# Block products from the third pair of column tiles on, with the products of the weights' own blocks first in a stage

## The chip, the core and the metric

The kernel runs on one core of a Trainium2 chip. The metric is the device time of one execution in microseconds (us). Four compute engines appear below: TensorE (PE, matrix products into the PSUM banks), VectorE (DVE), ScalarE (ACT) and GpSimd (POOL); SyncE (SP) issues most transfers. Each engine works through its own list of instructions in order and waits on semaphores for the others.

## What is computed

A trunk of two layers on 512 tokens of 1024 features, all in float32. Each layer is a half-step feed-forward block, a mixer (dilated attention and a convolution module, gated and merged) and a second half-step feed-forward block, each with an RMS norm ahead of it, and a final norm. The change is in the feed-forward blocks, of which there are four:

```python
def swiglu_ffn(h, w_up, w_down):
    a, b = jnp.split(h @ w_up, 2, axis=-1)
    return (jax.nn.silu(a) * b) @ w_down
...
    for l in range(DEPTH):
        x = x + 0.5 * swiglu_ffn(rmsnorm(x, ffn1_norm[l]), ffn1_w_up[l], ffn1_w_down[l])
        x = x + mixer(rmsnorm(x, mix_norm[l]), w_in[l], b_in[l], q_norm[l], k_norm[l],
                      w_attn_proj[l], conv_w[l], conv_b[l], conv_ln_g[l], conv_ln_b[l],
                      w_conv_proj[l], b_conv_proj[l], w_out[l], cos, sin)
        x = x + 0.5 * swiglu_ffn(rmsnorm(x, ffn2_norm[l]), ffn2_w_up[l], ffn2_w_down[l])
        x = rmsnorm(x, final_norm[l])
```

w_up is 1024 x 5632 (2816 columns for a, 2816 for b), w_down 2816 x 1024.

## The kernel before

**Number format.** PE multiplies in fp32r. To keep float32 accuracy each float32 matrix is split into a rounded part (hi, made by ACT) and the rest (lo, made by DVE as source less hi: L153 for a normal stage of weights, L167 elsewhere), and each product is three: hi x hi, hi x lo and lo x hi (`mm3`, L157 to L159). The activations are split once for a block, into xgh and xgl of eight k-tiles each.

**A feed-forward block** (`ffn`, L313) goes through the 22 column tiles of a and of b (128 columns each) in pairs m = 0, 2, 4, ..., in three parts of 8, 8 and 6 tiles; after each part come the products with w_down (ps_d). For each pair it needs the a half (two PSUM tiles ps_a) and the b half (two tiles ps_b, or the output o of a block product), then multiplies ps_a by R (the norm's factor, L338), applies Silu, multiplies by the b half (L341, L343) and splits the result into h.

**A normal pair** (`proj_cols`): two stages of weights of 512 KB, 48 products of 512 columns.

**A block product** (`proj7`, L282): the two column tiles and each pair of k-tiles form a 2 x 2 block matrix; the token halves (256 columns) and the k-tiles form the other one. Seven products of sums of blocks take the place of eight, so 84 products of 256 columns do the work of those 48. It too comes in two stages of 512 KB (`stage7`), each with two pairs q of k-tiles: DVE forms four sums of weight blocks (sm, L251 to L253), ACT rounds the raw block and the sums (hi, L166), DVE forms both rests (lo, L167). Of the seven products, numbers 0, 1 and 3 use the weights' own blocks, 2, 4, 5 and 6 their sums. They accumulate in four PSUM banks, given in `home`; at the end ACT and DVE combine the banks (L301 to L305). Before the change the b half of every pair but m = 0 is such a block product, and there it comes ahead of the a half: 10 in a feed-forward block, 40 in all.

**The sums of the activations** that the block products need are prepared once at the start of each `ffn`: DVE adds xgh and xgl again (L322, tile g), forms sums (`sums7`, L269 to L271, tile ts), ACT rounds them (Th) and DVE forms the rest (Tl). 

**The join of two stages.** At the end of a block the sums of squares of its output are added up over the partitions on PE (ps_ss, L198), made into a factor on DVE and ACT, spread by DVE onto a diagonal matrix dg (L212) and broadcast by PE (ps_bc, L214), from which ACT makes R (L220). ps_ss and ps_bc share one PSUM bank. Between the layers there are two ps_bc: the second one holds the final norm's factor, by which DVE rescales the eight x tiles within the next `ffn` (`deferred`, L778, called after pair m = 0). The pool of an `ffn` takes the memory that the pool before it gives back, dg's included.

**Buffers.** PSUM: three banks for ps_a (ps_mm), four for ps_b and the block products (ps_at), one for ps_ss and ps_bc (ps_st). Raw weights have two buffers, hi and lo four each, sm two.

**Order.** A tile scheduler that simulates a timeline fixes each engine's list when the program is built; stages of weights have a raised priority. What the list says is kept on the chip: an engine does not pass an instruction that waits.

In the code after the change, lines from L311 on have moved by one or two: L322 is L324, L338 is L340, L343 is L345, L778 is L780; of the block product's output, L301 to L305 are L302 to L306.

Of the kernel before, what the change touches and what calls it, by code (L numbers as in the profile page):

```python
# [44 lines left out]
def trunk(ctx: ExitStack, tc: tile.TileContext, A: dict, out: bass.AP):  # L45
# [8 lines left out]
    def ps_mm(name):  # L54
        return psp.tile([P, S], F32, tag="mm", name=name, bufs=3)

    def ps_st(name):
        return psp.tile([P, S], F32, tag="st", name=name, bufs=1)

    def ps_at(name):  # L60
        return psp.tile([P, S], F32, tag="at", name=name, bufs=4)
# [74 lines left out]
    def uniq(s):  # L136
        cnt[0] += 1
        return f"{s}_{cnt[0]}"
# [17 lines left out]
    def mm3(ps, ah, al, bh, bl, first, last):  # L156
        nc.tensor.matmul(ps, ah, bh, start=first, stop=False)  # L157
        nc.tensor.matmul(ps, ah, bl, start=False, stop=False)  # L158
        nc.tensor.matmul(ps, al, bh, start=False, stop=last)  # L159
# [80 lines left out]
    def stage7(pool, src):  # L240

        nk = src.shape[1]
        q = nk // 2
        m = nk * 256
        raw = wp.tile([P, 1024], F32, tag="raw", name=uniq("raw"), bufs=2)
        sm = pool.tile([P, 1024], F32, tag="sm", name=uniq("sm"), bufs=2)
        with tc.high_priority(offset=150):
            nc.sync.dma_start(raw[:, :m].rearrange("p (a n) -> p a n", a=nk), src)
            rv = raw[:, :m].rearrange("p (q e n) -> p e q n", q=q, e=4)
            sv = sm[:, :m].rearrange("p (e q n) -> p e q n", q=q, e=4)  # L250
            nc.vector.tensor_add(sv[:, 0:2], rv[:, 0::3], rv[:, 1][:, None].to_broadcast([P, 2, q, P]))  # L251
            nc.vector.tensor_add(sv[:, 2], sv[:, 1], rv[:, 0])
            nc.vector.tensor_add(sv[:, 3], sv[:, 2], rv[:, 2])  # L253
            f = []
            for t in (raw, sm):
                hi = wp.tile([P, 1024], F32R, tag="hi", name=uniq("hi"))
                lo = wp.tile([P, 1024], F32R, tag="lo", name=uniq("lo"))
                split_to(hi[:, :m], lo[:, :m], t[:, :m])
                p = "p (q e n) -> p e q n" if t is raw else "p (e q n) -> p e q n"
                f.append([x[:, :m].rearrange(p, q=q, e=4) for x in (hi, lo)])  # L260
        (rh, rl), (sh, sl) = f
        return [(rh[:, 0], rl[:, 0]), (rh[:, 2], rl[:, 2]), (sh[:, 3], sl[:, 3]), (rh[:, 3], rl[:, 3]),
                (sh[:, 1], sl[:, 1]), (sh[:, 2], sl[:, 2]), (sh[:, 0], sl[:, 0])]

    def sums7(pool, t2, h2, tag, bufs):

        tv = t2.rearrange("p k (h n) -> p (k h) n", h=2)
        w = pool.tile([P, 4, HT], F32, tag="w4", name=uniq("ts"), bufs=3)
        nc.vector.tensor_sub(w[:, 0:2], tv[:, 0::3], tv[:, 1:2].to_broadcast([P, 2, HT]))  # L269
        nc.vector.scalar_tensor_tensor(w[:, 2], w[:, 0], -1.0, tv[:, 3], op0=ALU.mult, op1=ALU.subtract)  # L270
        nc.vector.scalar_tensor_tensor(w[:, 3], w[:, 2], -1.0, tv[:, 2], op0=ALU.mult, op1=ALU.subtract)  # L271
        th = pool.tile([P, 4, HT], F32R, tag=tag, name=uniq("Th"), bufs=bufs)
        tl = pool.tile([P, 4, HT], F32R, tag=tag, name=uniq("Tl"), bufs=bufs)
        split_to(th, tl, w)

        def part(k, h):
            return tuple(x[:, h * HT:(h + 1) * HT] for x in h2[k])

        return [part(0, 0), part(1, 0), part(1, 1), (th[:, 3], tl[:, 3]),
                (th[:, 0], tl[:, 0]), (th[:, 2], tl[:, 2]), (th[:, 1], tl[:, 1])]  # L280

    def proj7(pool, src, c0, rhs, odd):  # L282

        if odd:
            bk = [ps_mm(uniq("ps_7")) for _ in range(3)] + [ps_st(uniq("ps_7"))]
        else:
            bk = [ps_at(uniq("ps_7")) for _ in range(4)]
        bv = [x.rearrange("p (h n) -> p h n", h=2) for x in bk]

        home = [(0, 0), (1, 0), (3, 0), (3, 1), (2, 0), (1, 1), (2, 1)]  # L290
        nq = len(rhs)
        for q0 in range(0, nq, 2):
            n_ = min(2, nq - q0)
            w = stage7(pool, src[:, 2 * q0:2 * (q0 + n_), c0:c0 + 256])
            for q in range(n_):
                for i in (0, 1, 5, 4, 6, 2, 3):
                    b, h = home[i]
                    mm3(bv[b][:, h], w[i][0][:, q], w[i][1][:, q], *rhs[q0 + q][i], q0 + q == 0 and h == 0, q0 + q == nq - 1 and (h == 1 or b == 0))
        o = pool.tile([P, 4, HT], F32, tag="w4", name=uniq("o7"), bufs=3)
        s1 = pool.tile([P, HT], F32, tag="s1", name=uniq("s1"), bufs=2)  # L300
        nc.scalar.activation(s1, bv[0][:, 0], AF.Copy)  # L301
        nc.vector.tensor_add(o[:, 0::3], bv[1], s1[:, None].to_broadcast([P, 2, HT]))  # L302
        nc.vector.tensor_add(o[:, 1:3], bv[2], o[:, 3:4].to_broadcast([P, 2, HT]))
        nc.vector.tensor_add(o[:, 3], bv[2][:, 0], o[:, 2])
        nc.vector.tensor_add(o[:, 1:3], bv[3], o[:, 1:3])  # L305
        return o.rearrange("p (k h) n -> p k (h n)", k=2)  # L306

    PARTS = ((0, 8), (8, 16), (16, 22))  # L311

    def ffn(l, w_up, w_down, xg, R, after, deferred=None):  # L313
        wu = w_up[l].rearrange("(k p) n -> p k n", p=P)
        wd = w_down[l].rearrange("(k p) n -> p k n", p=P)
        with tc.tile_pool(name=uniq("ffn"), bufs=4) as fp:
            few.add(id(fp))
            x7 = []
            for q in range(0, KD, 2):
                t2 = fp.tile([P, 2, S], F32, tag="t2", name=uniq("g2"), bufs=2)  # L320
                for j in range(2):
                    nc.vector.tensor_add(t2[:, j], xg[q + j][0].bitcast(F32), xg[q + j][1].bitcast(F32))  # L322
                x7.append(sums7(fp, t2, xg[q:q + 2], "T", 8))
            for m0, m1 in PARTS:  # L324
                h = []
                for m in range(m0, m1, 2):
                    pss = {}
                    for ab in ((0, 1) if m == 0 else (1, 0)):
                        if ab == 1 and m > 0:
                            o = proj7(fp, wu, FF + m * P, x7, False)  # L330
                            pss[1] = [o[:, 0], o[:, 1]]
                            continue
                        pss[ab] = [ps_mm(uniq("ps_a")) if ab == 0 else ps_at(uniq("ps_b")) for _ in range(2)]
                        proj_cols(wu, ab * FF + m * P, xg, KD, pss[ab])
                    t2 = fp.tile([P, 2, S], F32, tag="t2", name=uniq("t2"), bufs=2)
                    for j in range(2):
                        t = t2[:, j]
                        nc.vector.tensor_mul(t, pss[0][j], R)  # L338
                        nc.scalar.activation(t, t, AF.Silu)
                        if m > 0 and j == 1:  # L340
                            nc.vector.scalar_tensor_tensor(t, pss[1][j], -1.0, t, op0=ALU.mult, op1=ALU.mult)  # L341
                        else:
                            nc.vector.tensor_mul(t, pss[1][j], t)  # L343
                    h2 = split_to(*(fp.tile([P, 2, S], F32R, tag="h", name=uniq("h" + x), bufs=8) for x in "hl"), t2)
                    for j in range(2):  # L345
                        h.append(tuple(x[:, j] for x in h2))
                    if m == 0 and deferred is not None:
                        deferred()
                last = m1 == NF

                def take(k, src, f):
                    t = fp.tile([P, S], F32, tag="tmp", name=uniq("t"), bufs=5)
                    nc.vector.scalar_tensor_tensor(t, src, f, R, op0=ALU.mult, op1=ALU.mult)
                    nc.vector.tensor_add(xs[k], xs[k], t)
                    if last:
                        after(k, fp)

                wm = wd[:, m0:m1]
                for ts in ((0, 1), (2, 3), (4, 5), (6,), (7,)) if last else ((0, 1), (2, 3), (4, 5), (6, 7)):
                    pss = [(ps_at if ts[0] in (0, 4, 7) else ps_mm)(uniq("ps_d")) for _ in ts]  # L360
                    proj_cols(wm, ts[0] * P, h, m1 - m0, pss)
                    for k, ps in zip(ts, pss):
                        take(k, ps, 0.5)
# [492 lines left out]
```

## Time and profile before

| | us |
|---|---|
| median of 3 runs | 2684.32 (2680.71 to 2684.96) |
| the profiled execution | 2684.63 |
| its span | 2682.6 |
| PE busy in it | 2603.5 (97%) |
| DVE busy | 2018.0 (75%) |
| ACT busy | 1110.8 (41%) |
| mean granted clock of PE | 0.984 |

The busy time of an engine is the time in which it executes an instruction; PE's matmuls are pipelined, so the distance from one start to the next says more than the duration of one. The granted clock is the share of full speed that PE was given: 1.00 is 2.4 GHz, 0.50 is 1.2 GHz. In rows of the timeline, a bracket at the end tells how long the engine idled before the instruction and which instruction ended the idling. In rows, `ps` is a bank of a block product.

### The profile page before, as it was taken

What the parts mean: (1) busy time and instruction counts of PE and PEld (TensorE: products, weight loads), DVE (VectorE), ACT (ScalarE), POOL (GpSimd) and SP (SyncE); (2) the same over time, 40 slices, a digit from 0 to 9 for tenths busy, and PEclk for the clock granted to TensorE, in tenths of its full rate; (3) what the DMA queues carried; (4) which work ended last, traced back from release to release, by engine and by line L of the source; (5) the groups of instructions that cost most, each with busy time, mean ns of one, the idle gap of its engine ahead of it and who ended that gap; (6) DMA issues with size and microseconds to landing.
All of it is one profiled execution on the core that took longest, in us unless ns stands there. A gap on an engine that the chain in (4) does not pass through costs nothing.

```text
span 2682.6 us, 34833 instructions
## 1 busy us (share of the span) xinstructions
PE 2603.5 (97%) x13565; PEld 2180.7 (81%) x13565; DVE 2018.0 (75%) x3266; ACT 1110.8 (41%) x1664; POOL 110.7 (4%) x208
## 2 busy tenths in 40 slices
PE   7999999998999999999979999999989999999999
PEld 6888988776777778888858889887767778788887
DVE  6666669999986667666776666699999866676665
ACT  5333342243587234242433333422445873342334
POOL 1000000011011000000000000000010110000000
PEclk9999999999999999999989999999989999999999
DMA  3323233242333323232313232333323333232332
GB/s 126 114 91 108 85 114 106 80 121 88 107 108 113 114 79 103 87 112 92 104 47 110 87 111 90 111 103 91 110 86 119 111 124 106 63 118 87 110 94 79
DMA packets 245604, 268.89 MB, mean 100 GB/s; under 512 B 11624, under 2 KB 230128, under 8 KB 245440
## 3 DMA queue, kind: packets, MB, share of 16 engines
q1 hardware_dynamic: 233920, 234.91, 28.4%
q0 software_dynamic: 11504, 31.76, 4.0%
q8 instruction: 106, 1.74, 0.3%
q14 instruction: 58, 0.48, 0.1%
q10 hardware_dynamic: 16, 0.00, 0.0%
HBM read 251.75 MB, written 14.88 MB: 99 GB/s over the span
## 4 chain that ended last, share of the span: by engine, by line
PE 88%; DVE 10%; ACT 1%; issue 1%; DMA 0%; SPq 0%; DVEq 0%; ACTq 0%
PE ps_a L159 6%; PE ps_d L157 6%; PE ps_d L159 6%; PE ps_d L158 6%; PE ps_a L158 6%; PE ps_a L157 6%; PE ps L158 5%; PE ps L159 5%; PE ps L157 5%; PE ps_n L158 4%; PE ps_n L157 3%; PE ps_n L159 3%; DVE cv L618 2%; PE ps_S L526 1%; PE ps_pv L556 1%; PE ps_cp L158 1%
## 5 line engine op out<-in xcount | busy, mean ns | idle before, releaser
L152 ACT ACTIVATE hi<-raw 128x1024 fp32r<-128x1024 f32 (+1 forms) x368 | 378.5, 1039 | 611.5 <-PE ps_d L158 148.5
L153 DVE TENSOR_TENSOR lo<-raw,hi 128x1024 fp32r<-128x1024 f32 (+1 forms) x368 | 438.9, 1202 | 232.6 <-ACT hi L152 231.4
L618 DVE SCALAR_TENSOR_TENSOR cv<-u,cwc,cv 128x497 f32<-128x497 f32 (+14 forms) x480 | 339.0, 747 | 0.0
L157 PE MATMUL ps_a<-xgh,hi 128*128 128x512 f32 x704 | 275.1, 392 | 2.1 <-ACT xgh L174 2.1
L159 PE MATMUL ps_a<-xgh,lo 128*128 128x512 f32 x704 | 275.0, 392 | 1.8 <-DVE lo L153 1.8
L158 PE MATMUL ps_a<-xgl,hi 128*128 128x512 f32 x704 | 276.2, 392 | 0.1
L158 PE MATMUL ps_d<-hl,hi 128*128 128x512 f32 x704 | 272.6, 389 | 0.0
L159 PE MATMUL ps_d<-hh,lo 128*128 128x512 f32 x704 | 272.6, 389 | 0.0
L157 PE MATMUL ps_d<-hh,hi 128*128 128x512 f32 x704 | 270.6, 389 | 0.0
L158 PE MATMUL ps_n<-lo,xgh 128*128 128x512 f32 x576 | 229.0, 398 | 4.8 <-DVE lo L153 4.8
L159 PE MATMUL ps_n<-hi,xgl 128*128 128x512 f32 x576 | 226.0, 393 | 0.0
L157 PE MATMUL ps_n<-hi,xgh 128*128 128x512 f32 x576 | 215.0, 395 | 3.8 <-DVE tmp L481 3.8
L157 PE MATMUL ps<-Th,hi 128*128 128x256 f32 x640 | 182.3, 288 | 6.4 <-ACT Th L166 5.9
L158 PE MATMUL ps<-Tl,hi 128*128 128x256 f32 x640 | 183.9, 288 | 4.3 <-DVE Tl L167 4.3
L159 PE MATMUL ps<-Th,lo 128*128 128x256 f32 x640 | 182.0, 286 | 0.0
L166 ACT ACTIVATE hi<-sm 128x1024 fp32r<-128x1024 f32 x80 | 84.8, 1060 | 213.5 <-DVE sm L253 95.8
L159 PEld LDWEIGHTS ps_a<-xgh,lo 128*128 128x128 f32 x704 | 132.7, 189 | 31.1 <-DVE lo L153 3.1
L157 PEld LDWEIGHTS ps_a<-xgh,hi 128*128 128x128 f32 x704 | 133.0, 189 | 28.9 <-ACT xgh L174 2.5
L158 PEld LDWEIGHTS ps_a<-xgl,hi 128*128 128x128 f32 x704 | 132.8, 189 | 27.2 <-DVE xgl L175 0.8
L159 PEld LDWEIGHTS ps_d<-hh,lo 128*128 128x128 f32 x704 | 132.1, 188 | 27.5
L157 PEld LDWEIGHTS ps_d<-hh,hi 128*128 128x128 f32 x704 | 132.1, 188 | 27.4
L158 PEld LDWEIGHTS ps_d<-hl,hi 128*128 128x128 f32 x704 | 132.1, 188 | 27.4
(266 smaller groups left out, 5578.7 us busy)
## 6 DMA issues: line engine op xcount, KB each, us to landing
raw<-in_ffn_w_up_dram SPq DMA_DIRECT2D x176, 512.0 KB, 3.5
raw<-in_w_in_dram SPq DMA_DIRECT2D x88, 512.0 KB, 3.7
raw<-in_ffn_w_down_dram SPq DMA_DIRECT2D x76, 512.0 KB, 3.4
raw<-in_w_in_dram SPq DMA_DIRECT2D x96, 256.0 KB, 3.1
raw<-in_w_conv_proj_dram SPq DMA_DIRECT2D x16, 512.0 KB, 3.5
raw<-in_w_out_dram SPq DMA_DIRECT2D x16, 512.0 KB, 3.5
vd<-tmp POOLq DMA_DIRECT2D x24, 256.0 KB, 2.7
od<-ot POOLq DMA_DIRECT2D x24, 256.0 KB, 3.0
```

Source lines behind the costliest of these rows:

```text
L152: nc.scalar.activation(hi[:, :m], raw[:, :m], AF.Copy)
L153: nc.vector.tensor_sub(lo[:, :m], raw[:, :m], hi[:, :m].bitcast(F32))
L157: nc.tensor.matmul(ps, ah, bh, start=first, stop=False)
L158: nc.tensor.matmul(ps, ah, bl, start=False, stop=False)
L159: nc.tensor.matmul(ps, al, bh, start=False, stop=last)
L166: nc.scalar.activation(hi, src, AF.Copy)
L526: nc.tensor.matmul(pS[e][:, w * n + lo:w * n + hi], qkT[hp, i, b * P:(b + 1) * P], qkT[hp, 2 + i, k0 + lo:k0 + hi], start=True, stop=True)
L556: nc.tensor.matmul(pv[e * 64:(e + 1) * 64, i, b - b2, :], V[b + j][:, (hh * UH + h) * HD:(hh * UH + h + 1) * HD], PT[e][:, (nj * w + j) * ...
L618: nc.vector.scalar_tensor_tensor(a[:, t0:t1], u[k][:, t0 + d:t1 + d], cw(l, j, k), a[:, t0:t1], op0=ALU.mult, op1=ALU.add)
```

## The change

A constant M7 = 4 is added. In `ffn` the pairs m < 4 now are normal (the a half first, then the b half into ps_b), and block products begin at m = 4: 9 in a feed-forward block, 36 in all. The sign that goes with a block product's second tile (L341) follows. In `proj7` the loops within a stage are exchanged: the block products' number i runs outside, in the order 0, 1, 3, 5, 4, 6, 2, and the two pairs q of k-tiles run inside; which product opens and which closes a bank's accumulation follows. The transfers of weights on SP stay the same in number and order.

```diff
@@ -292,10 +292,11 @@
         for q0 in range(0, nq, 2):
             n_ = min(2, nq - q0)
             w = stage7(pool, src[:, 2 * q0:2 * (q0 + n_), c0:c0 + 256])
-            for q in range(n_):
-                for i in (0, 1, 5, 4, 6, 2, 3):
-                    b, h = home[i]
-                    mm3(bv[b][:, h], w[i][0][:, q], w[i][1][:, q], *rhs[q0 + q][i], q0 + q == 0 and h == 0, q0 + q == nq - 1 and (h == 1 or b == 0))
+
+            for i in (0, 1, 3, 5, 4, 6, 2):
+                b, h = home[i]
+                for q in range(n_):
+                    mm3(bv[b][:, h], w[i][0][:, q], w[i][1][:, q], *rhs[q0 + q][i], q0 + q == 0 and i in (0, 1, 3, 4), q0 + q == nq - 1 and i in (0, 5, 6, 2))
         o = pool.tile([P, 4, HT], F32, tag="w4", name=uniq("o7"), bufs=3)
         s1 = pool.tile([P, HT], F32, tag="s1", name=uniq("s1"), bufs=2)
         nc.scalar.activation(s1, bv[0][:, 0], AF.Copy)
@@ -308,6 +309,7 @@
 
 
 
+    M7 = 4
     PARTS = ((0, 8), (8, 16), (16, 22))
 
     def ffn(l, w_up, w_down, xg, R, after, deferred=None):
@@ -325,8 +327,8 @@
                 h = []
                 for m in range(m0, m1, 2):
                     pss = {}
-                    for ab in ((0, 1) if m == 0 else (1, 0)):
-                        if ab == 1 and m > 0:
+                    for ab in ((0, 1) if m < M7 else (1, 0)):
+                        if ab == 1 and m >= M7:
                             o = proj7(fp, wu, FF + m * P, x7, False)
                             pss[1] = [o[:, 0], o[:, 1]]
                             continue
@@ -337,7 +339,7 @@
                         t = t2[:, j]
                         nc.vector.tensor_mul(t, pss[0][j], R)
                         nc.scalar.activation(t, t, AF.Silu)
-                        if m > 0 and j == 1:
+                        if m >= M7 and j == 1:
                             nc.vector.scalar_tensor_tensor(t, pss[1][j], -1.0, t, op0=ALU.mult, op1=ALU.mult)
                         else:
                             nc.vector.tensor_mul(t, pss[1][j], t)
```

Three places in the engines' lists follow. The number behind a tile's name only tells instances apart.

PE at the feed-forward block 1 of layer 1, first block product (banks ps_1876, ps_1877) and the two ps_bc, before:

```order
L157 MATMUL ps_1876_11335<-xgh_10930,hi_11345 128x256
L158 MATMUL ps_1876_11335<-xgl_10931,hi_11345 128x256
L159 MATMUL ps_1876_11335<-xgh_10930,lo_11346 128x256
L214 MATMUL ps_bc_11133<-dg_11128,ones 128x512
L214 MATMUL ps_bc_11142<-dg_11137,ones 128x512
L157 MATMUL ps_1876_11335<-xgh_11006,hi_11401 128x256
L158 MATMUL ps_1876_11335<-xgl_11007,hi_11401 128x256
L157 MATMUL ps_1877_11336<-Th_11155,hi_11349 128x256
L159 MATMUL ps_1876_11335<-xgh_11006,lo_11402 128x256
```

There the two stand next to each other, 9 products into the block product. After, at the second normal pair (ps_b_11276 its fourth tile, ps_a_11214 its second):

```order
L157 MATMUL ps_b_11276<-xgh_10745,hi_11278 128x512
L158 MATMUL ps_b_11276<-xgl_10746,hi_11278 128x512
L159 MATMUL ps_b_11276<-xgh_10745,lo_11279 128x512
L214 MATMUL ps_bc_11020<-dg_11015,ones 128x512
L157 MATMUL ps_b_11276<-xgh_10808,hi_11278 128x512
L158 MATMUL ps_b_11276<-xgl_10809,hi_11278 128x512
...
L158 MATMUL ps_b_11276<-xgl_10974,hi_11308 128x512
L159 MATMUL ps_b_11276<-xgh_10973,lo_11309 128x512
L157 MATMUL ps_a_11214<-xgh_10734,hi_11216 128x512
L158 MATMUL ps_a_11214<-xgl_10735,hi_11216 128x512
L159 MATMUL ps_a_11214<-xgh_10734,lo_11217 128x512
```

The second ps_bc stood behind 9 products of the block product and now stands among the products of the second normal pair's b half; ps_a_11214 comes behind both ps_b tiles.

DVE at the same place, before (dg of the second ps_bc, the weights' sums, the activations' g, the rescales of x):

```order
L212 TENSOR_SCALAR dg_11137<-ident,rsr_11112 128x128 x4
L251 TENSOR_TENSOR sm_11340<-raw_11339 128x512
L322 TENSOR_TENSOR g_1841_11148<-xgh_10856,xgl_10857 128x512
L322 TENSOR_TENSOR g_1841_11148<-xgh_10867,xgl_10868 128x512
L322 TENSOR_TENSOR g_1845_11159<-xgh_10930,xgl_10931 128x512
L322 TENSOR_TENSOR g_1845_11159<-xgh_10943,xgl_10944 128x512
L251 TENSOR_TENSOR sm_11396<-raw_11395 128x512
L778 SCALAR_TENSOR_TENSOR x_81<-x_81,pcol,ps_bc_11142 128x512
L778 SCALAR_TENSOR_TENSOR x_82<-x_82,pcol,ps_bc_11142 128x512
```

The first operation of the new pool is there the weights' sum sm_11340. After:

```order
L212 TENSOR_SCALAR dg_11015<-ident,rsr_10990 128x128 x4
L153 TENSOR_TENSOR lo_11309<-raw_11307,hi_11308 128x1024
L324 TENSOR_TENSOR g_1821_11026<-xgh_10734,xgl_10735 128x512
L324 TENSOR_TENSOR g_1821_11026<-xgh_10745,xgl_10746 128x512
L324 TENSOR_TENSOR g_1825_11037<-xgh_10808,xgl_10809 128x512
L324 TENSOR_TENSOR g_1825_11037<-xgh_10821,xgl_10822 128x512
L251 TENSOR_TENSOR sm_11353<-raw_11352 128x512
L780 SCALAR_TENSOR_TENSOR x_81<-x_81,pcol,ps_bc_11020 128x512
L780 SCALAR_TENSOR_TENSOR x_82<-x_82,pcol,ps_bc_11020 128x512
```

One sum of weights (sm) ahead of the activations' g has gone behind them, and a rest (lo) of a normal stage stands there.

PE at the feed-forward block 2 of layer 0, from the last product of ps_b on into the first block product, before (pair m = 2, banks ps_1385 and ps_1386; hi_8309 and hi_8365 are the raw blocks' hi of the two stages, hi_8313 the sums' of the first):

```order
L159 MATMUL ps_b_8227<-xgh_8089,lo_8260 128x512
L157 MATMUL ps_1385_8299<-xgh_7848,hi_8309 128x256
...
L157 MATMUL ps_1386_8300<-xgh_7855,hi_8309 128x256
...
L157 MATMUL ps_1385_8299<-xgh_7925,hi_8309 128x256
...
L157 MATMUL ps_1385_8299<-xgh_8003,hi_8365 128x256
L158 MATMUL ps_1385_8299<-xgl_8004,hi_8365 128x256
L157 MATMUL ps_1386_8300<-Th_8127,hi_8313 128x256
L159 MATMUL ps_1385_8299<-xgh_8003,lo_8366 128x256
...
L158 MATMUL ps_1386_8300<-Tl_8128,hi_8313 128x256
L159 MATMUL ps_1386_8300<-Th_8127,lo_8314 128x256
```

The first two banks alone are worked on for a while there. After (pair m = 4; ps_1394, ps_1395 and ps_1397 are its first, second and fourth bank; of three products of one kind one is shown; hi_8383 is the raw blocks' hi, hi_8387 the sums'):

```order
L159 MATMUL ps_b_8301<-xgh_8028,lo_8334 128x512
L157 MATMUL ps_1394_8373<-xgh_7787,hi_8383 128x256
...
L157 MATMUL ps_1394_8373<-xgh_7864,hi_8383 128x256
...
L157 MATMUL ps_1395_8374<-xgh_7794,hi_8383 128x256
...
L157 MATMUL ps_1395_8374<-xgh_7872,hi_8383 128x256
...
L157 MATMUL ps_1397_8376<-Th_8066,hi_8383 128x256
...
L157 MATMUL ps_1397_8376<-Th_8077,hi_8383 128x256
...
L157 MATMUL ps_1395_8374<-Th_8066,hi_8387 128x256
```

Before, products of the first stage's sums (Th_8127 with hi_8313) stand among those of the second stage's own blocks. Now the first stage's own blocks, with numbers 0, 1 and 3 for both pairs q, come ahead of the first product of its sums (hi_8387).

## Rows read from the trace of the kernel before

**Rows 1.** The page: busy time of each engine; chain that ended last, by engine.
```profile
PE 2603.5 (97%) x13565; PEld 2180.7 (81%) x13565; DVE 2018.0 (75%) x3266; ACT 1110.8 (41%) x1664; POOL 110.7 (4%) x208
...
PE 88%; DVE 10%; ACT 1%; issue 1%; DMA 0%; SPq 0%; DVEq 0%; ACTq 0%
```

**Rows 2.** Timeline of PE: start, duration, instruction, tiles, shapes, [idle before, ended by].
```profile
32.23 0.40 PE L157 MATMUL ps_b<-xgh,hi 128*128 128x512 f32 x1
...
43.12 0.28 PE L157 MATMUL ps<-xgh,hi 128*128 128x256 f32 x1
...
71.23 0.28 PE L157 MATMUL ps<-xgh,hi 128*128 128x256 f32 x1
...
998.63 0.28 PE L157 MATMUL ps<-xgh,hi 128*128 128x256 f32 x1
...
1028.29 0.28 PE L157 MATMUL ps<-xgh,hi 128*128 128x256 f32 x1
...
1038.36 0.40 PE L157 MATMUL ps_a<-xgh,hi 128*128 128x512 f32 x1
...
1360.45 0.28 PE L157 MATMUL ps<-xgh,hi 128*128 128x256 f32 x1
...
1361.52 1.02 PE L214 MATMUL ps_bc<-dg,ones 128*128 128x512 f32 x2
1363.22 1.12 PE L214 MATMUL ps_bc<-dg,ones 128*128 128x512 f32 x2 [0.69 <-ACT R L220]
1377.72 0.58 PE L157 MATMUL ps<-xgh,hi 128*128 128x256 f32 x1 [13.37 <-ACT hi L166]
...
1407.65 0.28 PE L157 MATMUL ps<-xgh,hi 128*128 128x256 f32 x1
...
2330.19 0.28 PE L157 MATMUL ps<-xgh,hi 128*128 128x256 f32 x1
...
2360.45 0.28 PE L157 MATMUL ps<-xgh,hi 128*128 128x256 f32 x1
```

**Rows 3.** Windows: from:to, length, busy by engine (instructions), granted clock, DMA share, GB/s.
```profile
43.10:60.30 17.20, 13.57 (x85) 12.71 (x84) 15.08 (x21) 8.94 (x10) 0.00 (x0) 0.80 0.10 31
998.60:1016.90 18.30, 12.82 (x86) 11.74 (x85) 16.52 (x23) 10.21 (x13) 0.00 (x0) 0.91 0.16 52
1028.30:1038.40 10.10, 10.10 (x86) 10.10 (x85) 8.87 (x11) 5.55 (x7) 0.00 (x0) 1.00 0.30 87
1360.50:1395.60 35.10, 17.03 (x89) 13.95 (x88) 29.97 (x49) 12.45 (x15) 0.00 (x0) 0.66 0.10 30
1377.70:1389.30 11.60, 8.23 (x31) 7.06 (x32) 11.60 (x18) 4.90 (x6) 0.00 (x0) 0.50 0.23 72
```
The engines in each row are PE, PEld, DVE, ACT, POOL.

**Rows 4.** Timeline of DVE, columns as in rows 2.
```profile
990.88 0.69 DVE L251 TENSOR_TENSOR sm<-raw 128x512 f32<-128x512 f32 x1 [5.54 <-PE ps_bc L214]
...
1022.25 0.69 DVE L305 TENSOR_TENSOR o<-ps,o 128x512 f32<-128x512 f32 x1
...
1364.39 0.69 DVE L251 TENSOR_TENSOR sm<-raw 128x512 f32<-128x512 f32 x1 [3.35 <-PE ps_bc L214]
...
1368.01 3.38 DVE L778 SCALAR_TENSOR_TENSOR x<-x,pcol,ps_bc 128x512 f32<-128x512 f32 x5
...
1376.48 0.76 DVE L271 SCALAR_TENSOR_TENSOR ts<-ts,g 128x256 f32<-128x256 f32 x2
1377.15 1.23 DVE L167 TENSOR_TENSOR lo<-sm,hi 128x1024 fp32r<-128x1024 f32 x1
1378.29 2.50 DVE L322 TENSOR_TENSOR g<-xgh,xgl 128x512 f32<-128x512 f32 x4
...
1387.78 1.30 DVE L338 TENSOR_TENSOR t<-ps_a,R 128x512 f32<-128x512 f32 x2
```

**Rows 5.** Windows over the two mixers, columns as in rows 3.
```profile
379.70:975.00 595.30, 583.01 (x2835) 462.77 (x2834) 501.25 (x950) 276.65 (x505) 49.46 (x91) 0.98 0.35 105
1716.10:2306.60 590.50, 575.01 (x2836) 457.87 (x2836) 500.87 (x950) 273.90 (x503) 49.73 (x91) 0.99 0.35 106
```

## The prediction

> **What bounds the kernel now.** I read first the busy times and the chain of work that ended last: TensorE (PE) is busy 97% of the span and makes 88% of the chain, VectorE (DVE) 10% [rows 1]. So time is won where PE stands still or runs slowly. Next I read PE's own timeline around a block product in mid-kernel: the 84 products of 256 columns that begin at 1028.29 are followed at 1038.36 by the next pair's products, 10.07 us or 0.1199 us a product, with no wait [rows 2]; the window over them has the granted clock at 1.00, the 2.4 GHz level [rows 3]. A normal pair of column tiles, 48 products of 512 columns, goes from 32.23 to 43.12: 10.89 us, 0.2269 a product [rows 2]. A block product is thus 0.82 us cheaper than a normal pair where nothing waits, and an undisturbed pair m (block product and the ps_a pair behind it) takes 10.07 + 10.89 = 20.96 us.
>
> The first block product of each of the four FFNs is the exception. From its first product to the first of the next block product pass 28.11 us at FFN1 of layer 0 (43.12 to 71.23, place A), 29.66 at FFN2 of layer 0 (998.63 to 1028.29, B), 47.20 at FFN1 of layer 1 (1360.45 to 1407.65, C) and 30.26 at FFN2 of layer 1 (2330.19 to 2360.45, D) [rows 2]. Against 20.96 these are 7.15, 8.70, 26.24 and 9.30 us of stall, 51.4 in all. The windows show DVE nearly full there (15.08 of 17.20 us, 16.52 of 18.30, 29.97 of 35.10) and a granted clock of 0.80, 0.91 and 0.66 [rows 3]: PE waits for DVE, and after the waits it runs for a while at the lower level. What DVE does is the preparation of the activations' sums (L322, L269 to L271, L167), which can start only behind a ps_bc product of the stage before: its first operation at B comes at 990.88 after 5.54 us of idling for ps_bc, at C at 1364.39 after 3.35 [rows 4].
>
> **The change, part by part.** It makes normal pairs of the four block products at m = 2, leaves 36 of 40, and reorders the products inside a stage.
>
> The four pairs themselves: each costs 0.82 us more, 3.3 in all, if nothing waited. The Trainium skill ("TensorE: Matmul & The Clock Gate", "Back-to-back issue gap") gives a spacing of N/2.4 + 2.5 ns for warm isolated products, 215.8 and 109.2 ns here. By that estimate an exchanged pair would cost 48 x 215.8 - 84 x 109.2 ns = 1.19 us, and the sum below would be 1.5 us later. The rows, 227 and 120 ns, are 11 ns above it at both sizes and decide.
>
> A, B and D: two normal pairs back to back are 96 x 0.2268 = 21.77 us, if the first block product, now at m = 4, finds everything ready. At B: DVE starts at 990.88 as before. In the new order there stand, ahead of the rest (lo) of the block product's own first weights, 19 operations over 128x512 at 0.60 us (four L322 take 2.50 from 1378.29), 11 over 128x256 at 0.335 (two L271 from 1376.48 to 1377.15) and 7 rests at 1.14 (1377.15 to 1378.29) [rows 4]: 11.4 + 3.7 + 8.0 = 23.1, so it begins at 1014.0. PE wants it at 998.63 + 21.77 = 1020.40: 6.4 us spare. The sums' rest ends by the same count at 1017.4 and is wanted, behind 18 products, at 1022.6. The last ps_b eviction can begin only when its products are done, so it ends at about 1021.35; the bank it frees is touched 27 products in, at 1023.6, 2.3 us spare. D has B's order of instructions; at A the same count has the weights' rest ready near 59 and wanted at 64.9. I therefore take no wait: gains 28.11 - 21.77 = 6.34 at A, 7.89 at B, 8.49 at D. What is late next there is that last eviction.
>
> C keeps a wait, in another place. DVE's first L324 there has to stand behind the second ps_bc, as L251 did. Before, that product came 9 products of 256 columns into the stretch, after the first ps_bc: they ran at 1361.52 and 1363.22, 1.02 and 1.12 us [rows 2]. Now 42 products of 512 columns and the first ps_bc stand ahead of it: 1360.45 + 42 x 0.2268 + 1.02 = 1371.0, its end 1372.1, so DVE starts 7.8 us later than before. What it does until the first eviction of pair 0 (L338, now L340) is the same list less one rest, eight deferred rescales L778 (five in 3.38 us) included: 23.39 us before, from 1364.39 to 1387.78, hence 22.25 now [rows 4]. The eviction begins at 1394.4 and ends at 1395.1. It is wanted earlier: there are three ps_mm buffers, two held by pair 0 and one by the first column tile of m = 2, and so the second tile, ps_a_11214, put last by the scheduler, cannot begin. PE has done the 72 products before it at 1360.45 + 72 x 0.2268 + 2.14 = 1378.9 and then idles 16.2 us (13.37 before, on the weights' hi [rows 2]). Its 24 products follow, 5.44 us, at a clock that the idling will have lowered. What that costs is bounded by the windows: 0.09 of 18.30 us lost at B is 1.6; half of the 11.60 us at clock 0.50 after the 13.37 us wait at C is 5.8 [rows 3]. Here the work behind the wait is dense, as at A, where 0.20 of 17.20 is 3.4 [rows 3]; I take that. The next block product then begins at 1395.1 + 5.44 + 3.4 = 1404.0, 43.55 us after 1360.45. Gain at C: 47.20 - 43.55 = 3.65.
>
> The order inside a stage: the weights' sums are now wanted 18 products (2.16 us) into a stage of two, not 6 (0.72), and the fourth bank after 12 instead of 15. Neither is waited for in the steady block products, which already run at 0.1199 us and clock 1.00 with DVE at 8.87 of 10.10 us; the last read of a bank at B ends at 1022.25 + 0.69 = 1022.94, 5.35 us before the next block product [rows 2 to 4]. So it is worth nothing. Bounds: 0, and 36 x 3 x 0.12 = 13 us lost if the fourth bank were late by all that it is wanted earlier; the spare puts it at 0. The weights' transfers on SP keep their number and order.
>
> The scheduler also shifts some instructions in the mixers. The two before take 595.30 and 590.50 us for nearly the same work (2835 and 2836 products) [rows 5], which bounds such a shift by 4.8 us either way; PE waits at none of the places moved, so 0.
>
> Sum: 6.34 + 7.89 + 8.49 + 3.65 = 26.4 us, taken from the profiled execution (2684.63; its span is 2682.6): 2658.2. The median of the runs shown, 2684.32, is 0.3 lower, which I leave aside.
>
> **The rivals.** (1) C gains all: DVE's list starts early enough, or the second tile finds a buffer, and C also runs in 21.8 us: 2658.2 - 21.8 = 2636.4. Against it: the wait for ps_bc stands in DVE's row of before, and the order has the product later. 0.05. (2) C is dearer: the low clock takes the upper bound (+2.4) and the block product behind stalls as much as A's did (+7.15): up to 2667.8. For it: the second stage's weights and the last evictions pass DVE just then. 0.12. (3) The mixers' shift counts: 2653.4 or 2663.0. 0.13. (4) The stalls travel to m = 4. If DVE's preparation is not done when PE reaches that block product, the four pairs only add their 0.82: 2684.63 + 3.3 = 2687.9, slower. At B it decides when DVE is over 6.4 us later than I count, for instance because the extra evictions of pair 2 come ahead of the rests; against it is the count from rows. 0.07, of which 0.04 whole and 0.03 in half, which would end within 0.2%. (5) The reorder makes each block product wait for its fourth bank: up to 2658.2 + 13 = 2671. 0.03.
>
> **How the numbers follow.** The forecast has 0.60, and the rivals 0.05, 0.12, 0.13, 0.07 and 0.03. A measurement of this kernel tells about 0.2%, 5.4 us, from no change. All cases but the fourth are faster by more: 0.93 faster, 0.03 same, 0.04 slower. The range takes in the forecast, rivals 2 and 3 and a few us for the clock at A, B and D: 2649 to 2668; it leaves out rivals 1, 4 and 5.
>
> **What would show it.** In the changed profile the first block product of A, B and D begins with no idle time on PE before or in it, 21.8 us after 43.12, 998.63 and 2330.19 (shifted by the gains before), at clock 1.00. At C a row of ps_a L157 has some 16 us of idle put down to DVE's L340, and the clock is 0.50 for some us after it; DVE's first L324 waits for ps_bc until about 1372 less the 14.2 us gained before. Block products take 10.07 us as before. The forecast is wrong if the m = 4 block products of A, B or D wait on a lo, a Tl or an eviction, if C's idle time is gone or over 20 us, or if the mixers differ by over 5 us.

## The result and the profile after

The changed kernel takes 2654.36 us (median of 4 runs, 2654.13 to 2655.37), the kernel before took 2683.09 beside it (4 runs, 2680.71 to 2684.96). The ratio is 0.989, with an interval of 0.988 to 0.991: 1.1% faster. Forecast were 2658.2 (2649 to 2668), a gain of 26.4 us; the profiled executions are 29.3 us apart (2684.63 and 2655.37).

The page after, busy times and the chain of work that ended last [as rows 1]:

```profile
PE 2593.0 (98%) x13421; PEld 2168.9 (82%) x13421; DVE 1984.0 (75%) x3218; ACT 1100.8 (41%) x1651; POOL 110.8 (4%) x208
...
PE 92%; DVE 6%; ACT 1%; issue 1%; DMA 0%; SPq 0%; ACTq 0%
```

DVE's share of the chain has gone from 10% to 6%, PE's from 88% to 92%. The timeline of PE after at the four places (start, duration, instruction, shapes, idle before) answers to rows 2:

```profile
64.74 0.28 PE L157 MATMUL ps<-xgh,hi 128*128 128x256 f32 x1
...
990.68 0.39 PE L157 MATMUL ps_a<-xgh,hi 128*128 128x512 f32 x1
...
1012.45 0.28 PE L157 MATMUL ps<-xgh,hi 128*128 128x256 f32 x1
...
1344.60 0.40 PE L157 MATMUL ps_a<-xgh,hi 128*128 128x512 f32 x1
...
1349.15 1.02 PE L214 MATMUL ps_bc<-dg,ones 128*128 128x512 f32 x2
...
1355.03 1.02 PE L214 MATMUL ps_bc<-dg,ones 128*128 128x512 f32 x2
...
1379.09 0.79 PE L157 MATMUL ps_a<-xgh,hi 128*128 128x512 f32 x1 [16.22 <-DVE t L340]
...
1387.31 0.28 PE L157 MATMUL ps<-xgh,hi 128*128 128x256 f32 x1
...
1397.38 0.40 PE L157 MATMUL ps_a<-xgh,hi 128*128 128x512 f32 x1
...
2330.35 0.28 PE L157 MATMUL ps<-xgh,hi 128*128 128x256 f32 x1
```

At B the second normal pair runs from 990.68 to 1012.45, 21.77 us, and the block product begins at once. At C one row has a wait, 16.22 us for DVE's L340. The block product behind it takes 10.07 us (1387.31 to 1397.38), as every one of the 36 now does. The windows over the second normal pair at A, B, C and D, over the products behind C's wait, and over C's block product (columns as in rows 3):

```profile
43.00:64.70 21.70, 21.70 (x97) 18.00 (x96) 18.49 (x27) 10.70 (x12) 0.00 (x0) 1.00 0.30 97
990.70:1012.40 21.70, 21.70 (x97) 18.00 (x96) 20.59 (x30) 10.74 (x13) 0.00 (x0) 1.00 0.17 55
1344.60:1387.30 42.70, 26.48 (x101) 20.61 (x100) 32.60 (x54) 12.64 (x15) 0.00 (x0) 0.80 0.08 25
1379.10:1384.70 5.60, 5.60 (x13) 4.43 (x14) 5.29 (x7) 4.72 (x7) 0.00 (x0) 0.50 0.00 0
2308.60:2330.30 21.70, 21.70 (x97) 18.00 (x96) 20.60 (x30) 10.75 (x13) 0.00 (x0) 1.00 0.18 55
1387.30:1397.40 10.10, 10.10 (x86) 10.09 (x85) 6.95 (x9) 6.08 (x7) 0.00 (x0) 1.00 0.34 105
```

At A, B and D PE is busy all the time at the 2.4 GHz level, while DVE works through the same preparation as before (20.59 of 21.70 us at B). DVE's own timeline at C, and its last eviction at B:

```profile
1012.72 0.69 DVE L345 TENSOR_TENSOR t<-ps_b,t 128x512 f32<-128x512 f32 x1 [0.47 <-PE ps_b L159]
...
1356.09 2.50 DVE L324 TENSOR_TENSOR g<-xgh,xgl 128x512 f32<-128x512 f32 x4 [9.19 <-PE ps_bc L214]
...
1359.10 3.38 DVE L780 SCALAR_TENSOR_TENSOR x<-x,pcol,ps_bc 128x512 f32<-128x512 f32 x5
...
1363.00 2.06 DVE L780 SCALAR_TENSOR_TENSOR x<-x,pcol,ps_bc 128x512 f32<-128x512 f32 x3
...
1378.36 1.88 DVE L340 TENSOR_TENSOR t<-ps_a,R 128x512 f32<-128x512 f32 x3
```

Cut at the same events, the two profiled executions compare so (us):

| stretch | before | after | measured | forecast |
|---|---|---|---|---|
| start of the kernel to mixer 0 (A) | 379.73 | 373.24 | -6.49 | -6.34 |
| mixer 0 | 595.30 | 593.85 | -1.45 | 0 |
| FFN2 of layer 0 to the block product at m = 4 (B) | 53.26 | 45.36 | -7.90 | -7.89 |
| FFN1 of layer 1 to the block product at m = 4 (C) | 70.86 | 66.37 | -4.49 | -3.65 |
| mixer 1 | 590.44 | 589.18 | -1.26 | 0 |
| FFN2 of layer 1 to the block product at m = 4 (D) | 53.86 | 45.36 | -8.50 | -8.49 |
| the remaining stretches | 939.15 | 939.94 | +0.8 | 0 |
| span | 2682.6 | 2653.3 | -29.3 | -26.4 |

The remaining stretches are B's block product to FFN1 of layer 1 (308.50 and 308.49), C's to mixer 1 (308.50 twice) and D's to the end (322.15 and 322.95).

### The profile page after: what moved, and what is told of

Read it like the earlier page. It is cut to its first block, busy times and chain, and to the rows that moved or that the text cites. A ratio compares the mean times of both kernels' runs of the same rounds, so it can differ in the third digit from the quotient of the medians.

```text
span 2653.3 us, 34486 instructions
## 1 busy us (share of the span) xinstructions
PE 2593.0 (98%) x13421; PEld 2168.9 (82%) x13421; DVE 1984.0 (75%) x3218; ACT 1100.8 (41%) x1651; POOL 110.8 (4%) x208
## 4 chain that ended last, share of the span: by engine, by line
PE 92%; DVE 6%; ACT 1%; issue 1%; DMA 0%; SPq 0%; ACTq 0%
PE ps_a L158 6%; PE ps_a L159 6%; PE ps_a L157 6%; PE ps_d L158 6%; PE ps_d L157 6%; PE ps_d L159 6%; PE ps L159 5%; PE ps L158 5%; PE ps L157 5%; PE ps_n L158 4%; PE ps_n L157 4%; PE ps_n L159 4%; DVE cv L620 2%; PE ps_S L528 1%; PE ps_pv L558 1%; PE ps_cp L158 1%
## 5 line engine op out<-in xcount | busy, mean ns | idle before, releaser
L152 ACT ACTIVATE hi<-raw 128x1024 fp32r<-128x1024 f32 (+1 forms) x376 | 391.5, 1042 | 698.1 <-PE ps_d L158 156.1
L153 DVE TENSOR_TENSOR lo<-raw,hi 128x1024 fp32r<-128x1024 f32 (+1 forms) x376 | 451.1, 1200 | 252.0 <-ACT hi L152 251.1
L158 PE MATMUL ps<-Tl,hi 128*128 128x256 f32 x576 | 163.0, 283 | 0.0
L159 PE MATMUL ps<-Th,lo 128*128 128x256 f32 x576 | 163.0, 283 | 0.0
L157 PE MATMUL ps<-Th,hi 128*128 128x256 f32 x576 | 162.8, 283 | 0.0
L166 ACT ACTIVATE hi<-sm 128x1024 fp32r<-128x1024 f32 x72 | 76.4, 1061 | 184.7 <-DVE sm L253 76.0
```

The costliest lines, as they stand in the source:

```text
L152: nc.scalar.activation(hi[:, :m], raw[:, :m], AF.Copy)
L153: nc.vector.tensor_sub(lo[:, :m], raw[:, :m], hi[:, :m].bitcast(F32))
L166: nc.scalar.activation(hi, src, AF.Copy)
```

## Experiments

The theory that they test: at the four places the kernel before waited for DVE's list at the start of an `ffn`; the start at m = 4 gives that list one more pair of time, which is enough at A, B and D; the order inside a stage gives nothing; at C the wait moves to a ps_a buffer. The rivals: the order inside a stage carries part of the gain, or C's wait is for data of the block product.

**The order inside a stage alone.** The edit goes on the kernel before:

```diff
-            for q in range(n_):
-                for i in (0, 1, 5, 4, 6, 2, 3):
+            for i in (0, 1, 3, 5, 4, 6, 2):
+                b, h = home[i]
+                for q in range(n_):
```

> The kernel before with the changed order inside a stage alone; block products still begin at m = 2 (40 of them). Theory (the order inside a stage is worth nothing in the 36 steady block products, and at places A to D DVE's list sets the end, whatever the order on PE): 2683 within 4 us, block products of 10.07 us behind the first, the first one at A, B and D still 15 to 19 us long, C's 13.4 us wait still there. Rival (the order carries a good part of the gain): 2670 or less, with the waits of the first block product at A, B and D gone.

Measured: 2678.42 us (10 runs, 2677.20 to 2679.91) against 2684.46 (13 runs), ratio 0.9976 (0.9967 to 0.9985): 6 us faster. The timeline of PE shows waits left at B and C (D has two of B's again, 2.62 and 1.01 us):

```profile
993.94 0.58 PE L159 MATMUL ps<-xgh,lo 128*128 128x256 f32 x1 [2.62 <-DVE lo L167]
...
997.95 0.58 PE L158 MATMUL ps<-Tl,hi 128*128 128x256 f32 x1 [1.01 <-DVE Tl L167]
...
1368.22 0.58 PE L157 MATMUL ps<-xgh,hi 128*128 128x256 f32 x1 [13.36 <-ACT hi L166]
```

Outside the mixers this kernel is 10 us shorter than before: 4.9 in the first feed-forward block, 0.6, 2.1 and 2.2 in the others; its mixers are 3.6 us longer. The scheduler also puts products of the ps_a pair between the two halves of the first block product, so that PE has work while it waits. Neither expectation holds: the waits at B, C and D stay, but A's are nearly gone (0.40 and 0.57 us are left). With a start at m = 2 the order is worth something.

**The start at m = 4 alone.** The kernel after, with the old order inside a stage:

```diff
-            for i in (0, 1, 3, 5, 4, 6, 2):
-                b, h = home[i]
-                for q in range(n_):
+            for q in range(n_):
+                for i in (0, 1, 5, 4, 6, 2, 3):
```

> The changed kernel with the old order inside a stage; block products begin at m = 4. Theory (the start at m = 4 carries all of the gain): 2654.4 within 2 us, no wait at A, B and D, 16.2 us of waiting at C. Rival (the new order is needed for the first block product to find its sums ready): 1 to 4 us of waits in each first block product, 2658 to 2670.

Measured: 2649.81 us (2648.90 to 2650.38), ratio 0.9870 (0.9855 to 0.9885), 4.5 us less than the changed kernel. C's wait is the same:

```profile
1377.25 0.79 PE L157 MATMUL ps_a<-xgh,hi 128*128 128x512 f32 x1 [16.23 <-DVE t L339]
```

The feed-forward stretches agree with those of the changed kernel: 353.86 us twice from FFN2 of layer 0 to FFN1 of layer 1, 374.87 and 374.89 from there to mixer 1. So with a start at m = 4 the order inside a stage is worth nothing in the feed-forward blocks, and the start carries the whole gain. The 4.5 us lie in the mixers; the repetition below takes that up.

**Block products from m = 6 on.**

```diff
-    M7 = 4
+    M7 = 6
```

> The changed kernel with block products from m = 6 on (32 of them). Theory (nothing is left to gain at A, B and D, C's wait hangs on a ps_a buffer and not on the start of the block products): four more exchanged pairs at 0.82 us, 2654.4 + 3.3 = 2657.7, C's wait of 16.2 us still there. Rival (C's wait is for the block product's data and goes when that starts later): 2654.4 + 3.3 - 19 = 2639.

Measured: 2671.84 us (2668.10 to 2672.49), ratio 0.9949 (0.9935 to 0.9964), 14 us more than expected. Its row at C and its two mixers (windows):

```profile
1384.39 0.80 PE L157 MATMUL ps_a<-xgh,hi 128*128 128x512 f32 x1 [13.68 <-DVE t L340]
```

```profile
374.20:974.10 599.90, 582.49 (x2835) 461.97 (x2834) 501.56 (x950) 276.76 (x505) 49.88 (x91) 0.98 0.34 104
1701.20:2302.00 600.80, 580.36 (x2835) 459.44 (x2834) 501.71 (x950) 276.95 (x505) 49.89 (x91) 0.99 0.34 104
```

The wait at C stays, which speaks against the rival: the wait is not for data of the block product. It is 2.54 us shorter, which is what two L251 at 0.60 and four half-size operations at 0.335 take: with the block product two tiles later, the sums of its weights have left DVE's list ahead of the eviction. The exchanged pair costs its price where nothing waits (354.64 us for 353.86 in FFN2 of layer 0, +0.78, forecast 0.82). What was missed is the mixers: 1200.7 us together, against 1183.0 in the changed kernel.

**Out of the ring at C, block products from m = 6 there.** L340 writes to a tile t of the ring t2 (two buffers), which the preparation's four g tiles use too; so it stands behind all of them.

```diff
     def ffn(l, w_up, w_down, xg, R, after, deferred=None):
+        M7 = 4 if deferred is None else 6
...
-                t2 = fp.tile([P, 2, S], F32, tag="t2", name=uniq("g2"), bufs=2)
+                t2 = fp.tile([P, 2, S], F32, tag="t2" if deferred is None else "h", name=uniq("g2"), bufs=2 if deferred is None else 8)
```

> The changed kernel; in the feed-forward block at C alone the activations' g tiles take buffers of the tile h, which are free then, in place of the ring t2 that the evictions of ps_a also use, and block products begin there at m = 6. Theory (at C the eviction of ps_a stands behind the whole preparation because both share the ring of two buffers; the block product's data then need one more pair of time): the first eviction comes at about 17 us into the stretch, wanted at 18.4, so no wait for ps_a; the block product at m = 6 starts 45.7 us into the stretch, where now 63.7 us pass to the same point: 17.5 us gained, 2637. Rival (the wait comes from the late second ps_bc whatever the buffers): the wait of 16 us stays, 2655.

Measured: 2640.95 us (2639.95 to 2641.54), ratio 0.9838 (0.9822 to 0.9854): faster than both kernels. The window from the start of FFN1 of layer 1 to the block product, and that product's first row:

```profile
1320.80:1389.70 68.90, 68.90 (x309) 56.58 (x308) 49.99 (x81) 26.44 (x33) 0.00 (x0) 1.00 0.25 77
```

```profile
1389.74 0.28 PE L157 MATMUL ps<-xgh,hi 128*128 128x256 f32 x1
```

PE is busy all 68.90 us at clock 1.00: no wait and no low clock is left at C up to the block product, and inside that one wait of 0.25 us for a rest. FFN1 of layer 1 takes 356.99 us where it took 374.87, 17.9 less (17.5 forecast); the mixers take 1186.7, 3.7 more than in the changed kernel, so that 13.4 of it arrive in the median.

**Out of the ring at C alone, start still at m = 4.** The second line of the edit above without the first.

> The changed kernel with the g tiles out of the ring at place C alone, block products still from m = 4 on. Theory (at C DVE's whole list, not one buffer, is the limit: the evictions now come early, but the block product's sums come as late as before): no wait for ps_a; the block product starts about 24 us into the stretch, waits for its sums, whose last rest I count at 48 us, and ends near 50; the next one starts at 61, where it is 63.7 now: 1 to 4 us gained. Rival (the buffer alone is the cause): all of 18 us gained with the start at m = 4.

Measured: 2653.71 us (one run; 2687.80 for the kernel before beside it). PE at C:

```profile
1371.88 0.58 PE L157 MATMUL ps<-xgh,hi 128*128 128x256 f32 x1 [3.62 <-DVE t L345]
...
1378.13 0.58 PE L157 MATMUL ps<-xgh,hi 128*128 128x256 f32 x1 [3.31 <-ACT hi L166]
...
1381.95 0.58 PE L159 MATMUL ps<-xgh,lo 128*128 128x256 f32 x1 [1.87 <-DVE lo L167]
...
1403.92 0.28 PE L157 MATMUL ps<-xgh,hi 128*128 128x256 f32 x1
```

The wait for ps_a is gone, and in its place PE waits for an eviction and twice inside the block product for its data. FFN1 of layer 1 takes 370.53 us, 4.3 less than in the changed kernel, just above the 1 to 4 expected and far from 18. (The mixers take 3.4 more, 1186.4, so that little of it is left in the whole.) So at C the ring is one of two limits; behind it comes DVE's whole list, which needs one more pair of products as cover.

**More work in DVE's list.** The eight additions of an `ffn` are done twice, 4.8 us of DVE, in the changed kernel and in the kernel before:

```diff
                 for j in range(2):
-                    nc.vector.tensor_add(t2[:, j], xg[q + j][0].bitcast(F32), xg[q + j][1].bitcast(F32))
+                    for _ in range(2):
+                        nc.vector.tensor_add(t2[:, j], xg[q + j][0].bitcast(F32), xg[q + j][1].bitcast(F32))
```

> The changed kernel with the eight additions of the activations' g done twice: 8 x 0.6 = 4.8 us more on DVE in each feed-forward block. Theory (DVE's list sets the end at C alone; at A, B and D its spare is 5.1 us for the sums' rest and 2.3 us behind the last eviction): the wait at C grows by 4.8 from 16.2 to 21.0 us; A, B and D lose 0 to 2.5 us each. Rival 1 (DVE does not set the end at C): C unchanged at 43 us. Rival 2 (there is no spare): 4.8 us lost at each of the four.

> The kernel before with the eight additions of the activations' g done twice, 4.8 us more on DVE in each feed-forward block. Theory (before the change DVE's list set the end of the first block product at all four places): A, B, C and D each 4.8 us longer, 32.9, 34.5, 52.0 and 35.1 us from the first block product to the second, 19 us in all outside the mixers; beside it, the changed kernel lost 4.8 at C alone. Rival (PE's own order or the lower clock set the end at A, B and D): 1 to 3 us there.

Measured with the changed kernel: 2666.71 us (one run). PE's row at C and the windows of B and D:

```profile
1385.82 0.80 PE L157 MATMUL ps_a<-xgh,hi 128*128 128x512 f32 x1 [21.04 <-DVE t L341]
```

```profile
992.60:1014.30 21.70, 21.70 (x97) 18.00 (x96) 21.40 (x35) 10.38 (x12) 0.00 (x0) 1.00 0.22 70
2320.90:2342.60 21.70, 21.70 (x97) 18.00 (x96) 21.40 (x35) 10.37 (x12) 0.00 (x0) 1.00 0.22 70
```

C's wait grows from 16.22 to 21.04 us, by all of the 4.8; A, B and D lose nothing (353.87 us for 353.86 in FFN2 of layer 0), though DVE is busy 21.40 of 21.70 us at B and D. The whole loses 12.4 us, mostly because the mixers take 1191.4, 8.4 more. With the kernel before, 2709.55 us (one run, beside 2687.80), from the first block product to the second:

```profile
1004.44 0.28 PE L157 MATMUL ps<-xgh,hi 128*128 128x256 f32 x1
...
1040.32 0.28 PE L157 MATMUL ps<-xgh,hi 128*128 128x256 f32 x1
...
1372.48 0.28 PE L157 MATMUL ps<-xgh,hi 128*128 128x256 f32 x1
...
1425.63 0.28 PE L157 MATMUL ps<-xgh,hi 128*128 128x256 f32 x1
```

B takes 35.88 us for 29.66, C 53.15 for 47.20, A 32.51 for 28.11 and D 35.74 for 30.26: 4.4 to 6.2 us more at each of the four, 22 in all (19 expected; the clock is lower too: over the four stretches 0.84, 0.76, 0.68 and 0.81, before 0.88, 0.94, 0.75 and 0.94). DVE's list set the end at all four before and at C alone after. Of the spare that the prediction counted for the sums' rest (1017.4 to 1022.6, 5.2 us) at least 4.8 are there.

**The two starts at m = 4 once more, on one chip.**

> The changed kernel once more, beside the kernel with the start at m = 4 alone (4.5 us faster before, though its lists of instructions in the mixers are the same and its feed-forward blocks take the same 1470.3 us in the trace). Theory A (the 4.5 us are differences of the granted clock in the mixers that go with the program and not with the order inside a stage): 2654.4 within 1 us again, mixers together 1183 us, at lower clock for about 31 us of them. Theory B (a difference between chips or runs): the two come within 1 us of each other on the same chip.

> The start at m = 4 with the old order inside a stage once more, on the chip of the run before this one. Theory A: 2649.8 within 1 us, mixers together 1177 us, at lower clock for about 17 us of them. Theory B: within 1 us of the changed kernel.

Measured: 2653.69 us (2653.32 to 2654.70) and 2650.39 us (2649.62 to 2650.75), so 3.3 us apart, with ranges that don't meet. Windows over mixer 0 and mixer 1, first of the changed kernel, then of the start alone:

```profile
373.00:966.70 593.70, 582.07 (x2836) 462.32 (x2835) 501.69 (x950) 275.65 (x505) 49.49 (x91) 0.99 0.35 105
1695.20:2284.30 589.10, 577.04 (x2836) 459.19 (x2835) 501.52 (x950) 274.10 (x504) 49.51 (x91) 0.99 0.35 106
```

```profile
374.20:965.30 591.10, 578.71 (x2836) 460.30 (x2835) 501.47 (x950) 275.12 (x504) 49.49 (x91) 0.99 0.35 106
1694.10:2280.60 586.50, 575.67 (x2836) 457.94 (x2835) 501.16 (x950) 274.28 (x503) 49.50 (x91) 0.99 0.35 107
```

Each kernel repeats its own mixers within 0.3 us (593.85 and 593.64, 591.11 and 591.10 for mixer 0), the start alone on two different chips, though the two programs give every engine the same list there. In mixer 0 the difference lies where PE runs at the lower clock. Over the attention of mixer 0 PE has these windows in the changed kernel and with the start alone:

```profile
643.20:668.20 25.00, 19.35 (x113) 13.84 (x111) 25.00 (x56) 14.87 (x34) 1.85 (x3) 0.73 0.11 27
```

```profile
644.10:669.10 25.00, 17.94 (x123) 13.05 (x122) 25.00 (x56) 15.13 (x36) 2.39 (x4) 0.86 0.10 27
```

DVE is busy all 25 us in both, PE waits in several short pieces, by its rows for ACT, and the clock is 0.73 in one and 0.86 in the other. Followed product by product, the two come 1.2 us apart there and 1.6 more from 866 to 873 us, where products of ps_cp run at the lower clock in the changed kernel (first row) and not with the start alone (second row):

```profile
865.90:869.30 3.40, 3.40 (x10) 2.66 (x9) 2.00 (x4) 0.63 (x1) 1.08 (x2) 0.50 0.87 254
```

```profile
865.70:869.10 3.40, 3.40 (x17) 2.79 (x16) 2.12 (x4) 0.63 (x1) 1.08 (x2) 1.00 0.86 277
```

That makes up the 2.7 us of mixer 0. Three more programs have the same list in mixer 0: the ring freed with the start at m = 6, the ring freed alone, and the next experiment. They take 593.97, 593.93 and 593.67 us there, and the last of them, with the old order inside a stage, has the clock of the changed kernel over the attention:

```profile
642.70:667.70 25.00, 19.76 (x113) 14.21 (x113) 25.00 (x56) 15.08 (x34) 1.84 (x3) 0.73 0.11 28
```

That the mixers' difference goes with the program is shown (theory A), and it isn't the order inside a stage. The program with 591.1 is also the one in which mixer 0 starts latest, at 374.1 to 374.2 us against 372.8 to 373.2; whether that is the cause was not tested, and what makes PE fall to the lower clock at other points with equal lists stays open.

**Old order with the ring freed at C.** The edits of the fourth experiment with the old order inside a stage.

> The kernel with the g tiles out of the ring and block products from m = 6 on at place C, now with the old order inside a stage. Feed-forward blocks: 1451 us as with the new order, or up to 4 us more at C, where the sums are then wanted 1.4 us earlier in the first block product. The whole: 2640.9 if the mixers run as there (1187 us), down to 2632 if they run as with the start at m = 4 alone (1177).

Measured: 2643.57 us (2643.10 to 2646.82), ratio 0.9852 (0.9837 to 0.9867). FFN1 of layer 1 takes 357.92 us for 356.99 with the new order: 0.9 us, with one wait of 0.74 us for a rest of the sums in the first block product (0.25 with the new order). The mixers take 1189.8. Of the versions run, the one with the new order is the fastest.

## Why the prediction was right

- **What bounds the kernel.** Right: DVE's list at the start of an `ffn` was what PE waited for at all four places. The kernel before with 4.8 us more in that list lost 4.4 to 6.2 us at each.
- **A, B and D.** Right to 0.15 us. The second normal pair takes 21.77 us and nothing waits. The last ps_b eviction ends at 1012.72 + 0.69 = 1013.41 at B, 22.73 us into the pair; forecast were 22.72.
- **C keeps a wait in another place.** Right: 16.22 us for L340, as forecast. DVE starts 11.49 us into the stretch (1344.60 to 1356.09), 11.7 forecast, and L340 begins 22.27 us later, 22.25 forecast. The price of the lower clock was too high: the 24 products took 8.22 us (1379.09 to 1387.31) and not 5.44 + 3.4, so it cost 2.8. The taken row, A's, was the nearest of the three, and the measured price lies between B's 1.6 and it. Gain 4.49, forecast 3.65.
- **The order inside a stage: nothing.** Right for the change as it was made (353.86 us twice in FFN2 of layer 0). It holds because the start at m = 4 leaves nothing to wait for; by itself, with a start at m = 2, the order gives 10 us outside the mixers. The two parts of the change don't add up: they fill the same stalls. With the ring freed it is worth 0.9 us.
- **The mixers: 0, within 4.8 us.** This step was mis-sized. They gave 2.7 us here, about as much as the forecast missed, and over the versions that were profiled they went from 1177.3 to 1200.7 us together, within some tenths of a microsecond for the two that were repeated. The bound of 4.8 us, taken from the two mixers of one profile, held for this change but is too narrow for its neighbours (mixer 1 of the start at m = 6 took 600.8 us, 10.4 more than before), and the reason given, that PE waits at none of the places moved, doesn't cover it: equal lists gave 591.1 and 593.9 us. That the whole came out within the range is in this respect luck: with the 1200.7 us of that kernel it would have been 2672.

By an estimate from the spacing of isolated products in the Trainium skill ("TensorE: Matmul & The Clock Gate", "Back-to-back issue gap") an exchanged pair would cost 1.19 us. The pair exchanged at FFN2 of layer 0 in the kernel that starts at m = 6 cost 0.78, so the rows' spacing of 227 and 120 ns, which gives 0.82, holds here.

## What to carry to other kernels

A stretch in which a side engine prepares data needs cover on the main engine that is as long as its list; using the plainer form of the work there, though it is 0.8 us dearer, bought 6 to 8.5 us at each of three places. Where the cover suffices, look next for a buffer ring that the preparation shares with evictions: freed, and with one more pair of cover, it gave the remaining 18 us at C. And price two edits that fill the same stall once, not twice.

## What the runs showed of the hardware

The same lists of instructions in a mixer took 591.1 us in one program and 593.6 to 594.0 in four others, repeatably, with the granted clock over 25 us of the attention at 0.86 in the one and 0.73 in the others. A difference of 3 us between two builds of this kernel is therefore no evidence on an edit until the trace shows in which stretch it lies. After a wait of 16.22 us the dense products behind it ran at clock 0.50 for 5.6 us, which cost 2.8.
